# Five small changes of order and grain in a one-core hybrid mixer kernel: Inverse's stores and conversions, the scan's first level, the value rows' load, the opening

## The chip, the cores and the metric

The kernel runs on one core of a Trainium2 chip. The core has a tensor engine (PE) for matmuls and four others: the vector engine (DVE), the scalar engine (ACT), GpSimd (POOL) and the sync engine (SP). Each engine works through its own queue of instructions in the order in which they were written at build time, and waits on semaphores for what other engines deliver. SP, ACT and POOL also issue DMA transfers between the chip's memory (HBM) and the core's own memory; an issued transfer runs by itself on 16 DMA engines that all queues share, but the issuing instruction holds its engine's queue until it is accepted. The metric is the device time of one execution in microseconds (us); lower is better.

## The reference, cut to what matters

One layer over 128 context tokens and 2048 sample tokens of width 1024. The input projection feeds three branches: A, a bidirectional gated delta rule in chunks; B, a spatial-gating MLP; C, a Fourier mixing. Each is gated by a SiLU path, projected, merged with sigmoid gates and projected out.

```python
shift, scale, gate = ada_mod(c, w_ada, b_ada)
xn = rmsnorm(h, ln_g) * (1.0 + scale) + shift
proj = xn @ w_in                       # q k v, beta, decays, z_a, u_b, v_b, z_b, x_c, z_c, gates
# branch A, per chunk and head, both directions:
m = eye + beta * (k @ k.T) * dec_strict
sol = triangular_solve(m, rhs, lower=True, unit_diagonal=True)
s, o = lax.scan(step, s0, ...)         # state passed from chunk to chunk
o_a = rmsnorm(o, o_norm_g) * silu(z_a)
# branch B:
o_b = (u * (w_s @ rmsnorm(v, g_norm) + b_s)) * silu(z_b)
# branch C:
o_c = fft(x_c).real * silu(z_c)
merged = sum(sigmoid(gates_n) * (o_n @ w_branch_n))
y = rmsnorm(h + gate * (merged @ w_out), final_g)
```

## The kernel before, in words

Matmuls in full precision are made of three half-precision ones (high by high, low by high, high by low), so that a weight is split into `whi` and `wlo` and the activations into `xh` and `xl`. All of these go through one helper (`mm`, L239). Tokens are tiled as four tiles of 512 columns and one of 128 (`TBS`).

The work comes in stages: an opening (0 to 42 us), in which the adaLN maps are loaded and summed up; the z_a gate and the normalised activations (to 150 us); the q/k/v projection and the decays (to about 430 us); the spatial gating's v (to about 550 us); U and Z_B, whose product with v makes branch B (to 765 us); the Fourier branch (765 to 1050 us); the merges (to 2010 us); and the output projection. Branch A's work is laid in between these as a background generator, `delta()`. A pacer advances it by one step for each so many microseconds of dense work (`pace.tick`), and a list scheduler that simulates the engines then sets the order on each engine. A matmul of the background therefore stands at a fixed place in PE's queue; if its input is late, all dense work behind it waits. `tc.issue_after(x)` tells the scheduler not to place what follows ahead of the instruction x; on the instruction's own engine this is a matter of order alone.

Branch A goes in five groups of chunks (the context chunk, then four of four). For each chunk `prep` computes products and decays and leaves "late" steps: `late` writes an earlier step's result to HBM from ACT's queue, one step behind. For each group `base_inverse` (called Inverse here) inverts the 32-column base blocks of the triangular matrices, by 31 steps of two DVE operations over `E` (L1094, L1095). It then splits `E`, once straight and once transposed, into high and low halves in `XB`: the high part by ACT (L1100), the low part by DVE (L1101), 128 x 1024 each. The results go to HBM as `ei`, one store per direction: 64 partitions by 32 rows of 256 bytes. For groups 0 to 3 the stores are put in the list `extra`, and the next late step issues all that the list holds, on ACT's queue (L984); what remains at the end goes to SP's (L1407). For the last group SP issues them at once (L1109).

The scan loads `ei` and other results (SP, L1150 to L1156) into `ES`, `N` and others, has POOL copy parts of them (`T`, L1167), and runs the first level of the solve on PE as eight products `ES,N`.

In the gating stage, DVE multiplies each tile of U into a row `vrow` of branch B's values (L1529), POOL multiplies with the gate (`sg`, made by ACT at L1430 and DVE at L1432), and the next row of values is loaded one group ahead. In the Fourier stage `us`, `yT`, `X`, `Y` and `xc` are the transforms' intermediate tiles on ACT, DVE and POOL.

In the opening the order on DVE, ACT and PE is kept as written. `column_sums(b, g)` is one DVE operation over 1024 columns of an adaLN tile that has landed (`ab`), `block_pair` a product of it on PE, `row_copy` ACT's copy of this (`adr`), `turn_rows` PE's transposition of the copy, and `bound(i)` a few small DVE operations that bound the shift (0) or scale (1). `step0` and `step1` advance the first weights' splitting (`zhi`, `zlo`, `wsc`). The end of the opening is `bs` on DVE, then the scale matmul, then the first normalised tile.

Of the kernel before, what the change touches and what calls it, by code (L numbers as in the profile page):

```python
# [14 lines left out]
AF = mybir.ActivationFunctionType  # L15
ALU = mybir.AluOpType
# [19 lines left out]
FS = 4096.0  # L36
VS = 2048.0
ADA_D = (6, 7, 12, 13, 14, 15)
TBS = [(0, 512), (512, 512), (1024, 512), (1536, 512), (2048, 128)]
# [149 lines left out]
def hybrid_flow_kernel(ctx: ExitStack, tc: tile.TileContext, x_prompt, x_sample, state_delta, c, c_ctx, w_ada,  # L189
# [3 lines left out]
    G, SY = nc.gpsimd, nc.sync  # L193
    V, A, PE = [_InTurn(tc, e_) for e_ in (nc.vector, nc.scalar, nc.tensor)]
# [40 lines left out]
    mhalf = sb(cp, [P, 1], "mhalf")  # L235
    G.memset(mhalf, -0.5)

    def mm(out, l, r, start=True, stop=True):
        PE.matmul(out, l, r, start=start, stop=stop)  # L239

    def mm3(out, l, r, start=True, stop=True):

# [275 lines left out]
    def column_sums(b, g):  # L518
        V.scalar_tensor_tensor(spare(1), arrived[b], 1.0, rowc[g], ALU.mult, ALU.mult, accum_out=ada[:, b, g:g + 1])

    def block_pair(b):
        ps = bank(ps_d, [2, 256])
        for k in range(KT):
            mm(ps, scT[:, k, :], arrived[b + k // 4][:, k % 4 * 256:(k % 4 + 1) * 256], k == 0, k == KT - 1)
        return ps

    def turn_rows(b, adr):
        for k in range(2):
            PE.transpose(pa[:, b + k, :], adr[:, k * P:(k + 1) * P], ident[:2, :2])

    def row_copy(ps):
        adr = sb(p0p, [2, 256], "adr", bufs=1)
        A.copy(adr, ps)
        return adr
# [29 lines left out]
    p_ = block_pair(0)  # L564
# [3 lines left out]
    adr = row_copy(p_)  # L568
# [6 lines left out]
    p_ = block_pair(2)  # L575
# [5 lines left out]
    adr = row_copy(p_)  # L581
# [14 lines left out]
    step0()  # L596
    fetch_blocks(8, 9)
    turn_rows(4, adr)
    step0()
    step1()  # L600
    column_sums(13, 1)
    step1()
    step0()
    fetch_blocks(14, 10, 15, 11)
    p_ = block_pair(8)
    step1()
    step1()
    adr = row_copy(p_)
    turn_rows(8, adr)
    bound(0)  # L610
    column_sums(14, 0)
    column_sums(14, 1)
    p_ = block_pair(10)
    column_sums(15, 0)
    column_sums(15, 1)
    adr = row_copy(p_)
    turn_x0(4)
# [355 lines left out]
    def late(pairs=(), made=None):  # L973


        while owed and (made is None or len(owed) > 1):
            with tc.issue_after((made or owed[-1][1]).ins):
                for dst, src in owed.pop(0)[0]:
                    A.dma_start(dst, src)
        if made is not None:  # L980
            owed.append((list(pairs), made))
            with tc.issue_after(made.ins):
                while extra:
                    A.dma_start(*extra.pop(0))  # L984

    extra = []
# [86 lines left out]
    def base_inverse(g):  # L1073
        nt = len(GROUPS[g])
        nb = 16 * nt
        XB = sb(dq, [P, 2048], "XB")
        X, tmp = XB[:, 0:1024], XB[:, 1024:2048]
        E = sb(dq, [P, 1024], "E")
        if nt < 4:
            V.memset(X, 0.0)  # L1080
            V.memset(tmp, 0.0)
        b3 = lambda t_: t_.rearrange("p (j i) -> p j i", j=32)
        for d in range(2):
            SY.dma_start((X if d == 0 else tmp)[64 * d:64 * d + nb, :], ndD[g][d].rearrange("t h (b j) i -> (t h b) (j i)", b=4))
        for _ in range(8):
            yield 0
        V.tensor_copy(b3(X[64:P, :]), tmp[64:P, :].rearrange("p (i j) -> p j i", j=32))
        G.memset(E, 0.0)
        G.memset(E[:, 0:1024:33], 1.0)
        X3, E3 = b3(X), b3(E)  # L1090
        for k in range(31, 0, -1):
            n_ = 32 - k
            t3 = tmp[:, 0:k * n_].rearrange("p (j i) -> p j i", j=k)
            V.tensor_tensor(t3, X3[:, 0:k, k:k + 1].to_broadcast([P, k, n_]), E3[:, k:k + 1, k:32].to_broadcast([P, k, n_]), ALU.mult)  # L1094
            V.tensor_tensor(E3[:, 0:k, k:32], E3[:, 0:k, k:32], t3, ALU.subtract)  # L1095
            if k % 2 == 0:
                yield 1
        both = XB.bitcast(F16).rearrange("p (j l w c) -> p j l w c", j=32, l=2, w=2)
        for w, src in ((0, E3), (1, E.rearrange("p (i j) -> p j i", j=32))):
            A.activation(both[:, :, 0, w, :], src, AF.Copy, scale=FS)  # L1100
            V.scalar_tensor_tensor(both[:, :, 1, w, :], src, FS, both[:, :, 0, w, :], ALU.mult, ALU.subtract)  # L1101
            yield 1
        out = [(eD[g][d].rearrange("j t (y x) -> (t y) j x", x=128),
                both[64 * d:64 * d + nb].rearrange("p j l w c -> p j (l w c)")) for d in range(2)]
        if g < 4:
            extra.extend(out)
        for o_ in out:
            if g == 4:
                SY.dma_start(*o_)  # L1109
            yield 1  # L1110

    odd, wide, q_st, q_hi = [1], [], [], []

# [122 lines left out]
    def scan():  # L1236
# [20 lines left out]
        for _ in range(14):  # L1257
            yield 1
        for i in range(3):
            next(lev)  # L1260
            if i == 1:
                nlev = level(*order[1][::2])
                R2 = next(nlev)
            for _ in range(3):
                yield 1
# [248 lines left out]
    vst = ExitStack()  # L1514
    vp = pool(vst, "vp", 2)
    vnext = sb(vp, [P, NTOK], "vrow")
    SY.dma_start(vnext, vsD[0])
    for g in range(4):
        uw, zw = getw(2, 2)
        vrow = vnext  # L1520
# [366 lines left out]
```

## Time and profile before

| | |
|---|---|
| three runs, us | 2190.08, 2191.36, 2196.57; median 2191.36 |
| the profiled execution | 2189.06 us, of which the profile's span is 2186.8 |
| PE busy | 2108.4 us (96% of the span) |
| DVE, ACT, POOL busy | 1314.1, 1037.0, 704.8 us |
| mean granted clock of PE | 0.99 |
| DMA | 371.89 MB, mean 170 GB/s |

How to read it: times are those of one profiled execution, counted from the span's start. In a row of the timeline the first number is the start, the second the duration, then the engine, the line, the operation with output and inputs, and in brackets how long the engine sat idle ahead of it and who released it. "<-issue" means that the engine waited for nothing that the profile shows; ACTq and SPq are the queues' DMA issues, with the time that the issue took. Several like instructions in a row are one row ("x12"). A line such as L239 can be a helper's, so the tiles' names tell what is meant.

### The profile page before, as it was taken

To read this page: it belongs to the slowest core of one execution; us is meant where nothing else is said; L and a number is where in the kernel's file an instruction comes from. 1 tells how busy PE (TensorE), PEld (TensorE's weight loads), DVE (VectorE), ACT (ScalarE), POOL (GpSimd) and SP (SyncE) were. 2 spreads that over 40 slices of the span, in tenths; PEclk is the share of its full clock that TensorE was granted. 3 is DMA by queue.
4 is the path that set the end of the run, shared out by engine and by line. 5 is a ranking of instruction groups with operands and counts; after the bars stand their busy time and mean duration, and the time that the engine had idled before them with its cause. 6 is when DMAs were issued, how large, how long until landed. Compare 5 with 4: busy or idle time off the path is not lost. (4 is left out here: it accounts for less than half of the span.)

```text
span 2186.8 us, 42541 instructions
## 1 busy us (share of the span) xinstructions
PE 2108.4 (96%) x16249; PEld 1208.5 (55%) x16249; DVE 1314.1 (60%) x3039; ACT 1037.0 (47%) x2378; POOL 704.8 (32%) x869
## 2 busy tenths in 40 slices
PE   7999999999889999899899999899999999999998
PEld 4455444456445677777555555555655444444444
DVE  6656854389779697366665556765564544233454
ACT  5554744476555664445544445655553422223332
POOL 0321332233333432442322223355443222122543
PEclk9999999999999999999999999999999999999999
DMA  8625732277776743434655546766665533433542
GB/s 341 222 76 187 261 112 88 84 228 220 239 225 212 218 153 101 121 123 137 214 163 168 165 156 190 235 200 217 199 199 157 164 125 115 134 101 119 177 149 106
DMA packets 228011, 371.89 MB, mean 170 GB/s; under 512 B 38728, under 2 KB 125152, under 8 KB 225376
## 3 DMA queue, kind: packets, MB, share of 16 engines
q1 hardware_dynamic: 175424, 274.20, 39.9%
q0 software_dynamic: 12688, 51.27, 6.5%
q10 hardware_dynamic: 39696, 43.72, 6.0%
q8 instruction: 127, 2.08, 0.4%
q14 instruction: 76, 0.62, 0.1%
HBM read 241.48 MB, written 127.62 MB: 169 GB/s over the span
## 5 line engine op out<-in xcount | busy, mean ns | idle before, releaser
L239 PE MATMUL b<-xh,whi 128*128 128x512 f16 (+1 forms) x1920 | 650.9, 348 | 8.7 <-DVE sg L1432 6.0
L239 PE MATMUL b<-xl,whi 128*128 128x512 f16 (+1 forms) x1920 | 651.6, 348 | 0.0
L239 PE MATMUL b<-xh,wlo 128*128 128x512 f16 (+1 forms) x1920 | 650.7, 348 | 0.0
L239 PEld LDWEIGHTS <-whi 128*128 128x128 f16 x3904 | 356.3, 98 | 335.7 <-issue 16.6
L239 PEld LDWEIGHTS <-wlo 128*128 128x128 f16 x1952 | 191.3, 98 | 177.1 <-issue 2.8
L239 PE MATMUL b<-big,bhi 128*128 128x512 f16 (+1 forms) x960 | 250.7, 347 | 4.5 <-ACT big L1664 3.1
L1704 POOL TENSOR_TENSOR mrow<-mrow,sg 128x512 f32<-128x512 f32 (+1 forms) x80 | 94.6, 1183 | 281.5 <-DVE sg L1703 172.9
L239 PE MATMUL b<-big,blo 128*128 128x512 f16 (+1 forms) x480 | 162.9, 347 | 0.2 <-DVE blo L310 0.2
L1694 ACT ACTIVATE sg<-b,winv 128x512 f32<-128x512 f32 (+1 forms) x120 | 74.2, 618 | 132.8 <-PE b L239 132.3
L239 PEld LDWEIGHTS <-xh 128*128 128x128 f16 x1496 | 118.3, 99 | 28.9 <-issue 1.8
L239 PEld LDWEIGHTS <-bhi 128*128 128x128 f16 x960 | 86.4, 98 | 80.9 <-issue 4.2
L1703 DVE SCALAR_TENSOR_TENSOR sg<-b,binv,sg 128x512 f32<-128x512 f32 (+1 forms) x80 | 53.4, 667 | 128.5 <-PE b L239 120.3
L934 POOL TENSOR_TENSOR cy<-cy,raw 128x545 f32<-128x545 f32 (+1 forms) x48 | 65.3, 1387 | 183.8 <-ACT raw L933 183.8
L1167 POOL COPY T<-ES 32x256 f16<-32x256 f16 x68 | 28.1, 414 | 206.6 <-DMA ES<-ei 175.9
L239 PE MATMUL b<-wlo,xh 128*128 128x128 f16 x544 | 94.6, 221 | 0.0
L239 PE MATMUL b<-whi,xh 128*128 128x128 f16 x544 | 94.6, 221 | 0.0
L239 PE MATMUL b<-whi,xl 128*128 128x128 f16 x544 | 94.5, 221 | 0.0
L253 DVE CAST wscb<-wss 128x1 bf16<-128x1 f32 x89 | 13.6, 153 | 133.7 <-ACT wlo L297 55.4
L239 PE MATMUL b<-wohi,mh 128*128 128x512 f16 (+2 forms) x248 | 91.9, 372 | 0.0
L239 PE MATMUL b<-wolo,mh 128*128 128x512 f16 (+2 forms) x248 | 91.9, 372 | 0.0
L239 PE MATMUL b<-wohi,ml 128*128 128x512 f16 (+2 forms) x248 | 91.7, 372 | 0.0
L310 DVE SCALAR_TENSOR_TENSOR wlo<-wst,wsc,whi 128x1024 f16<-128x1024 f32 x52 | 70.6, 1360 | 32.7 <-ACT whi L309 32.6
(481 smaller groups left out, 4245.8 us busy)
## 6 DMA issues: line engine op xcount, KB each, us to landing
wst<-in_w_blk_dram SPq DMA_DIRECT2D x58, 512.0 KB, 6.1
qkv<-cy POOLq DMA_DIRECT2D x12, 1089.0 KB, 5.3
st<-br SPq DMA_DIRECT2D x48, 256.0 KB, 3.6
mrow<-mrg SPq DMA_DIRECT2D x18, 512.0 KB, 3.8
mrow<-mrg SPq DMA_DIRECT2D x16, 576.0 KB, 3.9
mrg<-mrow POOLq DMA_DIRECT2D x16, 576.0 KB, 3.8
dc<-dec SPq DMA_DIRECT2D x17, 512.0 KB, 4.7
kq<-qkv SPq DMA_DIRECT2D x34, 256.0 KB, 4.2
```

Of the source, the lines that this page charges most:

```text
L239: PE.matmul(out, l, r, start=start, stop=stop)
L253: V.tensor_copy(sb16, ss)
L310: w.low = V.scalar_tensor_tensor(w.lo, st, s, w.hi, ALU.mult, ALU.subtract)
L934: G.tensor_tensor(y[:, c0:c1], y[:, c0:c1], raw[:, 1 + c0:1 + c1], ALU.mult)
L1167: G.tensor_copy(T16[rows(a0, b), :, :, b], ES[0:32, :, 2 * a0 + b, :, wT])
L1694: A.activation(sg, ps, AF.Sigmoid, scale=gw.inv)
L1703: V.scalar_tensor_tensor(sg, ps, binv[:, 1:2], sg, ALU.mult, ALU.mult)
L1704: G.tensor_tensor(mr, mr, sg, ALU.add)
```

## The change

Five parts. **Opening**: the column sums (13, 1) and (14, 0) and the second advance of the weights' steps are written at other places, and `bound(0)` is written near the end. **Conversions**: each of Inverse's four conversions is made in two halves of 16 of the 32 rows, both kinds for the first half, then both for the second, so that there are four pieces on ACT and four on DVE per group. **Stores**: each store is made in two halves likewise. A late step issues at most one from the list, not all of it; the last group's go out as soon as a half is ready, one direction on SP's queue and the other on ACT's. **Scan**: the first three steps of the first level may not be placed ahead of the newest matmul written so far. **Value rows**: the first load of a row comes tile by tile, in five transfers.

```diff
-        PE.matmul(out, l, r, start=start, stop=stop)
+        newest[0] = PE.matmul(out, l, r, start=start, stop=stop)
...
     turn_rows(4, adr)
+    column_sums(13, 1)
     step0()
     step1()
-    column_sums(13, 1)
-    step1()
-    step0()
     fetch_blocks(14, 10, 15, 11)
     p_ = block_pair(8)
     step1()
+    step0()
+    column_sums(14, 0)
+    adr = row_copy(p_)
     step1()
-    adr = row_copy(p_)
     turn_rows(8, adr)
-    bound(0)
-    column_sums(14, 0)
     column_sums(14, 1)
     p_ = block_pair(10)
+    step1()
     column_sums(15, 0)
+    bound(0)
     column_sums(15, 1)
...
-                while extra:
+                if extra:
                     A.dma_start(*extra.pop(0))
...
-        for w, src in ((0, E3), (1, E.rearrange("p (i j) -> p j i", j=32))):
-            A.activation(both[:, :, 0, w, :], src, AF.Copy, scale=FS)
-            V.scalar_tensor_tensor(both[:, :, 1, w, :], src, FS, both[:, :, 0, w, :], ALU.mult, ALU.subtract)
-            yield 1
-        out = [(eD[g][d].rearrange("j t (y x) -> (t y) j x", x=128),
-                both[64 * d:64 * d + nb].rearrange("p j l w c -> p j (l w c)")) for d in range(2)]
-        if g < 4:
-            extra.extend(out)
-        for o_ in out:
-            if g == 4:
-                SY.dma_start(*o_)
-            yield 1
+        for j0 in (0, 16):
+            js = slice(j0, j0 + 16)
+            for w, src in ((0, E3), (1, E.rearrange("p (i j) -> p j i", j=32))):
+                A.activation(both[:, js, 0, w, :], src[:, js], AF.Copy, scale=FS)
+                V.scalar_tensor_tensor(both[:, js, 1, w, :], src[:, js], FS, both[:, js, 0, w, :], ALU.mult, ALU.subtract)
+                yield 1
+            out = [(eD[g][d][js].rearrange("j t (y x) -> (t y) j x", x=128),
+                    both[64 * d:64 * d + nb, js].rearrange("p j l w c -> p j (l w c)")) for d in range(2)]
+            if g < 4:
+                extra.extend(out)
+            else:
+                SY.dma_start(*out[0])
+                A.dma_start(*out[1])
...
         for i in range(3):
-            next(lev)
+            with tc.issue_after(newest[0].ins):
+                next(lev)
...
-    SY.dma_start(vnext, vsD[0])
+    for t0, tn in TBS:
+        SY.dma_start(vnext[:, t0:t0 + tn], vsD[0][:, t0:t0 + tn])
```

The lines behind the change move by two to five (L1430 becomes L1434, L1101 becomes L1105).

The first place is ACT's queue in the second group's late steps, where the trace of before has the stores at 637 to 648 us. `ei` are Inverse's stores, `n`, `qk` and `kT` the late steps' own, `sg` is a gate of the dense work. Before:

```order
L1063 ACTIVATE n_864_6753<-n_863_6751 128x512
L984 DMA ei_3926<-XB_5743 64x32x128
L979 DMA n_7_3836<-n_857_6689 128x1024
L984 DMA ei_3926<-XB_5743 64x32x128
L1063 ACTIVATE n_870_6795<-n_869_6793 128x512
L979 DMA n_7_3853<-n_859_6704 128x1024
L979 DMA qk_7_3870<-n_864_6753 128x1024
L1430 ACTIVATE sg_6784<-b_6759,winv_5724 128x512
```

And after, at the same place:

```order
L1065 ACTIVATE n_864_6765<-n_863_6763 128x512
L986 DMA ei_3926<-XB_5751 64x16x128
L981 DMA n_7_3836<-n_857_6699 128x1024
L986 DMA ei_3926<-XB_5751 64x16x128
L1065 ACTIVATE n_870_6808<-n_869_6806 128x512
L981 DMA n_7_3853<-n_859_6714 128x1024
L986 DMA ei_3926<-XB_5751 64x16x128
L1434 ACTIVATE sg_6797<-b_6772,winv_5732 128x512
L981 DMA qk_7_3870<-n_864_6765 128x1024
```

Three halves now stand ahead of `sg` where two wholes stood, and one `qk` store has gone behind it; the fourth half follows the last `qk` store, twelve rows further on.

The second place is DVE's queue at the end of the last Inverse, at 873 to 881 us in the trace of before. `yT` are operations of the Fourier stage. Before:

```order
L1094 TENSOR_TENSOR XB_9660<-XB_9660,E_9661 128x31
L1095 TENSOR_TENSOR E_9661<-E_9661,XB_9660 128x31
L1547 TENSOR_SCALAR X_1091_8275<-b_10217,X_1091_8275 128x4x63
L1602 TENSOR_SCALAR X_1091_8275<-X_1091_8275 128x4x63 x2
L1101 TENSOR_SCALAR XB_9660<-E_9661,XB_9660 128x32x32 x2
L1616 TENSOR_TENSOR yT_9544<-b_10238,us_10263 128x7x32
L1617 TENSOR_TENSOR yT_9544<-b_10238,us_10263 128x7x32
L1432 TENSOR_SCALAR sg_10300<-b_10275,zs_9546,sg_10300 128x512
```

And after:

```order
L1096 TENSOR_TENSOR XB_9688<-XB_9688,E_9689 128x31
L1097 TENSOR_TENSOR E_9689<-E_9689,XB_9688 128x31
L1621 TENSOR_TENSOR yT_9569<-b_10266,us_10291 128x7x32
L1622 TENSOR_TENSOR yT_9569<-b_10266,us_10291 128x7x32
L1105 TENSOR_SCALAR XB_9688<-E_9689,XB_9688 128x16x32 x4
L1436 TENSOR_SCALAR sg_10328<-b_10303,zs_9571,sg_10328 128x512
```

The conversions are four pieces instead of two, and `yT` stands ahead of them; `sg` stays behind them.

The third place is PE's queue at the scan's start, 893 to 910 us in the trace of before. Before:

```order
L239 MATMUL b_10536<-xl_94,whi_8874 128x128
L239 LDWEIGHTS wlo_8875
L239 MATMUL b_10536<-xh_93,wlo_8875 128x128
L239 LDWEIGHTS N_1274_10475
L239 MATMUL b_10749<-ES_10477,N_1274_10475 128x32
L239 LDWEIGHTS xh_93
L239 MATMUL b_10572<-whi_9648,xh_93 128x128
```

And after, from 336 rows further on (168 weight loads and 168 matmuls):

```order
L241 MATMUL b_10710<-wlo_9674,xh_93 128x128
L241 LDWEIGHTS xl_94
L241 MATMUL b_10710<-whi_9673,xl_94 128x128
L241 LDWEIGHTS N_1274_10509
L241 MATMUL b_10783<-ES_10511,N_1274_10509 128x32
```

The first of the eight products `ES,N` stood ahead of 168 matmuls of dense work, and the other seven behind them; now all eight stand behind.

More of the change, by code (lines that the diff above doesn't have):

```diff
@@ L236, in hybrid_flow_kernel @@
     G.memset(mhalf, -0.5)
+    newest = [None]
     def mm(out, l, r, start=True, stop=True):
-        PE.matmul(out, l, r, start=start, stop=stop)
+        newest[0] = PE.matmul(out, l, r, start=start, stop=stop)
     def mm3(out, l, r, start=True, stop=True):
```

## The prediction

> **What bounds the kernel now.** I read the busy times first, then the tensor engine's (PE's) waits by stage, then the order of work around each wait. The page's row of busy times says that PE is the bound; the rest of the span, 2186.8 less 2108.4, is 78.4 us in which it is idle.
>
> ```profile
> PE 2108.4 (96%) x16249; PEld 1208.5 (55%) x16249; DVE 1314.1 (60%) x3039; ACT 1037.0 (47%) x2378; POOL 704.8 (32%) x869
> ```
>
> The change leaves PE's matmuls as they are, so it can act only on those 78 us (or add to them). The view of PE's waits, here from 575 to 935 us (rows: total, times, longest), names what it waits for; most of these rows belong to places that the change touches. The two rows after "..." are the same view from 545 to 575 us.
>
> ```profile
> PE b L239 <- DVE sg L1432: 8.6, 3, 5.5
> PE b L239 <- POOL T L1167: 5.0, 1, 5.0
> PE b L239 <- ACT yT L1637: 2.8, 2, 1.9
> PE b L1030 <- DVE tok L1014: 1.8, 1, 1.8
> PE b L239 <- DVE X L1602: 1.2, 1, 1.2
> PE b L1030 <- DVE ss L1004: 0.9, 1, 0.9
> PE b L239 <- POOL X L1601: 0.6, 1, 0.6
> ...
> PE b L239 <- DVE vrow L1529: 2.4, 1, 2.4
> PE b L239 <- DVE T L1032: 1.1, 1, 1.1
> ```
>
> **The change part by part.** Gains are in us of PE's idle time; each has a value and, in brackets, its ends.
>
> Opening order. DVE's column sums (xl<-ab) take 1.2 us each, and four of them run one after the other up to 39.1 us, after which PE's scale matmul still waits for bs:
>
> ```profile
> 27.25 0.16 DVE L182 TENSOR_SCALAR wsc<-b 128x1 int32<-128x1 int32 x1 [2.02 <-PE b L182]
> 32.47 1.28 DVE L182 SCALAR_TENSOR_TENSOR zlo<-wst,wsc,zhi 128x1024 f16<-128x1024 f32 x1 [1.15 <-ACT zhi L182]
> 37.84 1.22 DVE L182 SCALAR_TENSOR_TENSOR xl<-ab,rowc 128x1024 f16<-128x1024 f32 x1
> 40.02 0.16 PE L182 MATMUL b<-bs,ones 128*128 128x1 bf16 x1 [1.20 <-DVE bs L182]
> ```
>
> Two of the four move ahead, into the holes of 2.02 and 1.15 us; the tail is shorter by 2 x 1.22 = 2.4 us, and the three small operations of the first bound move into it (about 0.16 each by the 27.25 row, so 0.5). That leaves 2.0 (0, if the two tiles have not landed by then, to 2.4).
>
> Value rows by tile. The first load of 1088 KB is issued at 551.89; DVE, then idle 5.50 us, gets it at 558.10, and the next two operations on it are followed by two conversions of Inverse, behind which T (L1032) stands:
>
> ```profile
> 551.89 0.33 SPq L1517 DMA_DIRECT2D vrow<-vs  x1
> 558.10 1.41 DVE L1529 SCALAR_TENSOR_TENSOR vrow<-b,winv,vrow 128x512 f32<-128x512 f32 x2 [5.50 <-DMA vrow<-vs]
> 559.42 3.73 DVE L1101 SCALAR_TENSOR_TENSOR XB<-E,XB 128x1024 f16<-128x1024 f32 x2
> st<-br SPq DMA_DIRECT2D x48, 256.0 KB, 3.6
> ```
>
> A piece of 256 KB, the size of the st<-br loads (3.6 us), lands near 555.5, 2.6 us earlier. That covers the whole 2.4; the 1.1 behind T remains in part, since the conversions still stand ahead of T and now begin 2.6 us earlier. Together 2.0 of 3.5 (0 to 3.5): I stay under the sum because the second operation now waits for a second piece. SP issues four rows more, 4 x 0.33 = 1.3 us; the second group's rows, queued behind them, are read only after the first group's five gates, and those cover it.
>
> Stores in halves. At 637 us two stores of 512 KB of Inverse's result (ei, L984), in rows of 256 B, go out on ACT's queue among the late steps' own stores (L979). The issue of a store stands until the queue has room, and what stands behind it on ACT waits:
>
> ```profile
> 637.71 0.67 ACTq L984 DMA_DIRECT2D ei<-XB  x1
> 640.15 1.71 ACTq L984 DMA_DIRECT2D ei<-XB  x1
> 641.98 5.44 ACTq L979 DMA_DIRECT2D n<-n  x1
> 648.23 0.69 ACT L1430 ACTIVATE sg<-b,winv 128x512 f32<-128x512 f32 x1 [5.64 <-issue]
> 649.75 0.59 PE L239 MATMUL b<-xh,whi 128*128 128x512 f16 x1 [5.49 <-DVE sg L1432]
> 638.00:644.00 6.00, 6.00 (x70) 4.84 (x69) 3.25 (x5) 2.48 (x5) 0.76 (x1) 1.00 0.83 123
> ```
>
> So a gate (sg) that was ready waited 5.64 us behind an issue, and PE 5.49. After the change three halves stand ahead of sg and the fourth behind it, after the last qk. The window's last column gives 123 GB/s while the stores ran, hence 256 KB/123 = 2.1 us a half. Three halves from 637.71 are through by 644.1, against 646.3 for four; and an issue is let go before its data is through, so sg should start at 643 to 644 instead of 648.2. PE wants its result at 649.75 - 5.49 = 644.26, DVE's step between; I take 4.7 (0, if the third half stands as long as the store at 641.98, to 5.5).
> At 736 us the same happens in the next group:
>
> ```profile
> 736.38 4.62 ACTq L984 DMA_DIRECT2D ei<-XB  x2
> 741.18 3.17 ACTq L979 DMA_DIRECT2D n<-n  x1
> DMA to landing us min/median/max: 2.4/3.5/4.9
> ```
>
> Here PE pays only the 1.8 of tok, which ACT's delay hands on through DVE: 1.5 (0 to 1.8). In the third group (823 us) PE does not wait; two halves now go to SP's queue after prep's end, ahead of the load that feeds the last Inverse. Taken at nothing, as the conversions of that Inverse come only at 874; if it is late all the way, 2 x 2.1, which the new waits below take in. A rule speaks against halves: the Trainium skill, "DMA: Bandwidth & Descriptors", section Bandwidth, advises at least 1 MiB a transfer, since each carries a fixed part. By the formula of that page's anatomy section (2.0 us and bytes over 436 GB/s, fitted on the other kind of queue) a half is an estimated 2.6 us, three are 7.8, and this term would be 3.3 for 4.7, the sum 1.4 smaller. The trace has 3.5 us as the median landing of a whole (the page's estimate 3.2), so the page is close there; for a half no row exists.
>
> Conversions in four pieces. DVE's and ACT's conversions of Inverse's result, ten of 1024 columns each, become twenty of 512:
>
> ```profile
> L1101 DVE SCALAR_TENSOR_TENSOR XB<-E,XB x10: 1225/1906/1949, 559.4 to 876.8; 128x1024 f16<-128x1024 f32 x10
> 811.72 2.93 ACT L1100 ACTIVATE XB<-E 128x1024 f16<-128x1024 f32 x2
> 814.67 1.91 DVE L1101 SCALAR_TENSOR_TENSOR XB<-E,XB 128x1024 f16<-128x1024 f32 x1 [0.64 <-ACT XB L1100]
> 815.13 0.83 PE L239 MATMUL b<-cf,Y 128*128 128x128 f16 x12 [1.87 <-ACT yT L1637]
> 818.26 0.39 PE L239 MATMUL b<-cf,X 128*128 128x128 f16 x2 [1.18 <-DVE X L1602]
> 876.81 1.92 DVE L1101 SCALAR_TENSOR_TENSOR XB<-E,XB 128x1024 f16<-128x1024 f32 x1 [0.66 <-ACT XB L1100]
> 881.79 0.37 ACT L1612 COPY us<-b 128x256 f32<-128x256 f32 x1
> 881.16 0.29 PE L239 MATMUL b<-cf,X 128*128 128x128 f16 x2 [2.64 <-DVE sg L1432]
> 882.39 1.44 PE L239 MATMUL b<-cf,Y 128*128 128x128 f16 x12 [0.94 <-ACT yT L1637]
> ```
>
> At 811 to 818 ACT's yT stood behind 2.93 us of conversions and DVE's X behind 1.91; PE lost 0.93 + 1.87 + 0.62 + 1.18 = 4.6 (ss, yT, POOL's X, DVE's X). In the new order us, yT, X and T come before the conversions on ACT, and yT, X and T before them on DVE: 3.2 (0 to 4.6), since ss doesn't move and the last X still follows. At 876 to 882 PE lost 2.64 + 0.94 = 3.6. There yT comes ahead of the four pieces, but sg stays behind them, and a wait is added: ACT's queue issues two halves itself, the second only when DVE's fourth piece is done; sg stands between the two, X, us and the yT that PE waits for behind both. DVE's conversions end now at 876.81 + 1.92 = 878.7; if the four pieces end there too, that yT comes after four operations of ACT of about 0.4 (the us row), near 880.4 and not 882.4; PE's sg comes earlier than that. Less 0.5 for a fourth piece that ends later, 1.5 (-1, if ACT waits long for it, to 3.6). Pieces of 512 columns should take the 0.70 of a vrow operation (1.41/2), so 2.8 a group against 2 x 1.225: 0.35 more, 0.7 in the two groups where PE waits; in the others DVE's idle time hides it.
>
> Scan's first level. Its first matmul stands ahead of 168 dense ones that don't need it, and waits for the loads of the scan, POOL's copy last:
>
> ```profile
> 897.96 0.84 POOL L1167 COPY T<-ES 32x256 f16<-32x256 f16 x2 [3.48 <-DMA ES<-ei]
> 898.81 0.18 PE L239 MATMUL b<-ES,N 128*128 128x32 f16 x1 [4.96 <-POOL T L1167]
> 910.05 0.33 PE L239 MATMUL b<-ES,N 128*128 128x32 f16 x7
> ```
>
> Put behind those 168 (898.81 to 910.05, 11.2 us), it is reached at 898.81 - 4.96 + 11.2 = 905.1, 6.3 us after the copies end at 898.8. The wait goes: 5.0 (0 to 5.0). PE's arrival may move ahead of the loads by all that the 811 to 882 stretch gains, 4.7, before it is late again.
>
> New waits. The order of ACT, DVE and SP shifts by some places from 550 to 880 us. Nothing in the trace shows what then comes last; between no wait and three of the size of tok's 1.8 I take one, 1.8.
>
> Sum: 2.0 + 2.0 + 4.7 + 1.5 + 3.2 + 1.5 + 5.0 = 19.9, less 0.7 and 1.8: 17.4. The profiled execution took 2189.06 us (2.3 outside its span) and would come to 2171.7; it lies 2.3 under the median of the three runs, 2191.36, from which I count: 2174.0.
>
> **The rivals.**
> The halves stand as long as wholes: three at the 3.5 us of a whole end at 637.71 + 10.5 = 648.2, where sg starts now, and both store terms (6.2) are gone: 2180.2. For it speaks that the bytes and their 256 B rows stay the same, against it the 123 GB/s.
> The conversions' waits come back under other names, the 4.7 of 811 to 882 gone: 2178.7. For it: sg still stands behind four pieces; against it: yT and X don't. With the first rival together: 2184.9.
> The first level doesn't move or waits again: 2179.0. For it would speak loads later by over 6.3 us; SP's half-stores of group 3 come ahead of them, at 2.1 each too little.
> Slower: every half on ACT's queue is paid by PE in full. There are twelve large ones (4, 4, 2, 2); at 2.1 each 25.6 us instead of the 5.5 + 1.8 paid now, +18.3, against 11.2 from the other terms (after the 2.5 of costs): 2198.5. It decides from (7.3 + 11.2)/12 = 1.5 us paid per half. The 5.64 row speaks for it; against it, that the 640.15 issue took 1.71 with PE still covered, and that work of ACT's own now lies between the halves.
>
> **How the numbers follow.** Forecast 0.55; stores 0.14, conversions 0.12, both 0.06, first level 0.06, slower 0.07. Best ends together give 26.4, 2165.0; the range goes to 2164 and up past both rivals to 2188, which leaves out the slower case. No change that can be told is 0.3%, 6.6 us: both rivals together fall on that line, and with a tail of the others it gets 0.08; slower 0.07, faster 0.85.
>
> **What would show it.** PE's wait for sg near 650 under 1 us; ACT's gap before sg without an issue of 5 us; PE's row for ES,N without a wait for POOL; vrow's wait under 3 us on DVE; bs on DVE 2 us earlier; less than 2 us of waits for yT and X before each of the last two Inverse ends. Wrong would be an n or ei issue over 3 us on ACT with sg behind it, a wait of PE above 2 us with a new releaser between 550 and 890, or ES copies that end after PE's 168 matmuls.

## The result, and the profile after

Twenty runs of each kernel: 2190.03 us before (2184.19 to 2196.57) and 2180.49 us after (2174.15 to 2186.51), medians. The ratio is 0.9954, with a 95% interval of 0.9944 to 0.9964, so the change saves 10 us (8 to 12), where 17.4 were forecast. The profiled execution of the changed kernel took 2174.15 us, the fastest of its twenty; its trace, with a span of 2172.3 us, lies 14.5 us under that of before, and some 5 us of this are that execution's luck.

Where the 14.5 us come from is seen in the view of busy times by stretch. After the stretch and its length stands PE's busy time; the last three columns are the granted clock, the DMA share and GB/s. First the kernel before, then the changed one:

```profile
0.00:45.00 45.00, 33.02 (x171) 18.65 (x172) 24.08 (x59) 22.21 (x40) 2.59 (x10) 0.97 0.94 361
45.00:545.00 500.00, 494.00 (x3118) 256.77 (x3117) 331.41 (x610) 274.93 (x524) 139.39 (x165) 0.99 0.49 165
545.00:935.00 390.00, 360.93 (x3407) 245.65 (x3406) 293.93 (x733) 207.03 (x583) 137.65 (x181) 0.97 0.59 180
935.00:1680.00 745.00, 720.37 (x6915) 448.72 (x6914) 450.35 (x1163) 383.20 (x999) 270.75 (x375) 1.00 0.58 181
```
```profile
0.00:45.00 45.00, 36.27 (x181) 20.26 (x182) 26.67 (x63) 24.97 (x44) 2.54 (x10) 0.96 0.97 387
45.00:545.00 500.00, 495.17 (x3135) 257.98 (x3134) 333.55 (x626) 275.85 (x538) 140.96 (x168) 1.00 0.49 166
545.00:935.00 390.00, 368.21 (x3569) 250.00 (x3568) 299.13 (x749) 212.41 (x595) 141.51 (x191) 0.99 0.59 182
935.00:1680.00 745.00, 718.77 (x6803) 444.66 (x6801) 446.42 (x1150) 379.21 (x985) 269.01 (x367) 1.00 0.59 181
```

PE's idle time is the length less the busy time. It falls from 18.0 to 13.6 us up to 545 us, from 29.1 to 21.8 from 545 to 935, and rises from 31.3 to 34.1 after that (the rest of the span included): 78.4 before, 69.4 after, 9.0 less. The other 5.5 us are busy time, 2108.4 before and 2102.9 after for the same 16249 matmuls. That is the clock, and it was no term of the prediction, which let the change act on the 78 us of idle time only: the third row's granted clock is 0.97 before and 0.99 after. It isn't this pair alone: the mean granted clock is 0.994 over the twenty runs of the changed kernel, and 0.990 over those of the kernel before that ran beside the later experiments. The kernel before in steps of two us behind its stall at 650 shows how:

```profile
648.00:650.00 2.00, 0.25 (x1) 0.10 (x1) 0.77 (x2) 1.77 (x10) 0.22 (x1) 0.50 1.20 329
650.00:652.00 2.00, 2.00 (x6) 0.76 (x5) 1.49 (x3) 2.00 (x10) 1.90 (x2) 0.50 0.81 297
652.00:654.00 2.00, 2.00 (x8) 0.67 (x6) 1.11 (x3) 2.00 (x6) 1.97 (x4) 0.61 0.77 184
654.00:656.00 2.00, 2.00 (x11) 0.94 (x10) 0.16 (x1) 0.90 (x4) 1.69 (x4) 1.00 0.96 313
```

After this wait PE's clock is granted at half, and stays low for some 4 us after work has come back: 6 matmuls in two us, then 8, then 11. Busy time times the clock that was missing, 2.00 x 0.50 + 2.00 x 0.39 and so on, gives 1.9 us for this stall on top of its 5.5. Added up over the span this is 15.9 us before, in eight places, and 8.0 after, in five; from 545 to 935 us it is 8.4 and 3.3. This working takes all busy time as slowed by the clock, which is an estimate; its 7.9 less is somewhat more than the 5.5 by which the busy time fell.

What PE waits for from 545 (in this view 575) to 935 us after the change:

```profile
PE b L241 <- DVE sg L1436: 3.3, 4, 1.6
PE b L999 <- issue: 3.2, 1, 3.2
PE b L241 <- ACT yT L1642: 2.8, 1, 2.8
PE b L241 <- DVE T L1034: 2.0, 3, 1.1
PE b L999 <- DVE n L1047: 1.7, 1, 1.7
PE b L241 <- DVE X L1607: 1.1, 2, 0.6
PE b L241 <- DVE yT L1622: 1.0, 1, 1.0
```

The 5.5 us for sg (now 0.47 there) and the 5.0 for POOL's T are gone. A wait of 3.2 has come, and 2.8 for yT stand where 2.6 for sg stood. The stores themselves do what was forecast, at 633 to 639 us:

```profile
633.01 0.67 ACTq L986 DMA_DIRECT2D ei<-XB  x1
634.42 1.22 ACTq L986 DMA_DIRECT2D ei<-XB  x1
636.99 1.63 ACTq L986 DMA_DIRECT2D ei<-XB  x1
638.66 0.69 ACT L1434 ACTIVATE sg<-b,winv 128x512 f32<-128x512 f32 x1 [2.29 <-PE b L241]
638.69 2.49 ACTq L981 DMA_DIRECT2D qk<-n  x1
```

ACT's gate sg no longer waits for an issue but for PE's own matmuls; PE then waits 0.47 us for it, not 5.49. The store that stands longest, qk with 2.49, has sg in front of it.

### The profile page after: what moved, and what is told of

It is laid out like the page before. It is cut to its first block, busy times and chain, and to the rows that moved or that the text cites. A ratio compares the mean times of both kernels' runs of the same rounds, so it can differ in the third digit from the quotient of the medians.

```text
span 2172.3 us, 42588 instructions
## 1 busy us (share of the span) xinstructions
PE 2102.9 (97%) x16249; PEld 1204.3 (55%) x16249; DVE 1314.2 (60%) x3049; ACT 1037.8 (48%) x2388; POOL 704.2 (32%) x869
```

## The experiments

All ratios are to runs of the kernel before on the same chip, with 95% intervals. The table gives, beside the median of each kernel's runs, the time of its one profiled execution and two readings of that execution from 545 to 935 us: PE's idle time, and the time lost to the half clock, worked out as above (where the windows start moves this by up to 0.4). Where the profiled execution lies far from the median, the two readings are those of an uncommonly fast or slow one.

| kernel | median, us | ratio | profiled, us | idle | lost to the clock |
|---|---|---|---|---|---|
| before | 2190.0 | | 2189.1 | 29.1 | 8.4 |
| opening alone | 2188.4 | 0.9997 (0.9985 to 1.0008) | 2183.1 | 29.3 | 6.9 |
| value rows alone | 2191.0 | 1.0001 (0.9990 to 1.0011) | 2190.8 | 27.1 | 9.1 |
| scan's first level alone | 2190.0 | 1.0004 (0.9993 to 1.0014) | 2191.2 | 28.9 | 8.1 |
| conversions alone | 2196.5 | 1.0029 (1.0017 to 1.0041) | 2190.4 | 31.4 | 7.1 |
| stores alone | 2180.8 | 0.9960 (0.9948 to 0.9971) | 2180.8 | 20.4 | 1.7 |
| the whole change | 2180.5 | 0.9954 (0.9944 to 0.9964) | 2174.2 | 21.8 | 3.3 |
| the whole change again | 2177.4 | 0.9945 (0.9925 to 0.9965) | 2170.9 | 20.9 | 1.5 |
| stores and conversions | 2181.2 | 0.9959 (0.9944 to 0.9973) | 2188.9 | 25.7 | 4.6 |
| whole, without the conversions | 2186.4 | 0.9979 (0.9966 to 0.9991) | 2184.9 | 23.5 | 8.5 |
| whole, halves on two queues | 2178.5 | 0.9953 (0.9938 to 0.9967) | 2178.2 | 22.2 | 2.9 |
| whole, last stores whole | 2176.4 | 0.9944 (0.9926 to 0.9961) | 2175.3 | 21.6 | 1.6 |
| whole, last halves on SP | 2186.0 | 0.9974 (0.9958 to 0.9990) | 2186.6 | 27.4 | 5.1 |
| whole, two queues and last whole | 2180.2 | 0.9953 (0.9938 to 0.9969) | 2183.9 | 23.2 | 4.0 |

The parts don't add: only the stores, made alone, save time that can be told, and they save nearly all of it; the conversions, made alone, cost 6 us (4 to 9).

**The opening alone.**

```diff
     turn_rows(4, adr)
+    column_sums(13, 1)
...
-    bound(0)
-    column_sums(14, 0)
...
     column_sums(15, 0)
+    bound(0)
```

> Only the opening's order is changed. First theory (the tail of column sums is shorter by two, and all behind it moves up): the first normalised matmul starts 2.0 us earlier than before (42.6 to about 40.6), and the time is 2 us less. Rival (the z_a stage behind it is paced by transfers, so the gain is given back): the same 2.0 us at 42 us, but PE's waits for DMA or DVE between 45 and 150 us grow by as much, and the time is the same.

Measured: the first normalised matmul starts at 40.1 us, not 42.6, 0.5 of it because the first transfers landed earlier; in the changed kernel it is 39.9. The rival's z_a stage doesn't take it back: PE's idle time up to 545 us is 15.1 us here and 18.0 before, and has a mean of 15.1 (13.5 to 16.3) in the eight profiles with the new order and 17.0 (15.1 to 18.8) in the six without. Later in this kernel's trace the waits for yT grew (4.4 us at 831, 2.8 at 896). The time doesn't tell 2.0 us from none. What follows: the opening's 2 us are there at 42 us and, in the mean, still at 545; whether they last to the end is not settled.

**The value rows alone.**

```diff
-    SY.dma_start(vnext, vsD[0])
+    for t0, tn in TBS:
+        SY.dma_start(vnext[:, t0:t0 + tn], vsD[0][:, t0:t0 + tn])
```

> Only the first row of values is loaded tile by tile. First theory (after the changed kernel's trace): vrow's wait of 2.4 us goes, but T, behind Inverse's conversions, becomes the wait: 0 to 1 us less. Rival (the prediction's): both together fall from 3.5 to 1.5 us: 2 us less.

Measured: vrow's wait is gone, T's waits are 0.93 and 0.64; the two together fall from 3.5 to 1.6. The time is the same; 1.9 us is below what its interval can tell. In the changed kernel it is 2.0 that remain, again T's:

```profile
556.21 0.23 PE L241 MATMUL b<-T 128*128 128x128 f16 x1 [1.59 <-ACT T L1033]
557.43 0.77 PE L241 MATMUL b<-T 128*128 128x128 f16 x11 [0.45 <-DVE T L1034]
```

A new wait of 1.06 us at 574, for tok behind an operation of Inverse on DVE, comes with the conversions and not with this part: it stands in all eight profiles with conversions in pieces and in none of the six without. What follows: the wait moved to T, as the prediction said of a part of it; 1.5 to 1.9 of the 3.5 us are saved on the spot, and the time can't show whether they last.

**The scan's first level alone.**

```diff
-            next(lev)
+            with tc.issue_after(newest[0].ins):
+                next(lev)
```

> Only the scan's first level is kept behind the newest matmul. First theory: the wait of 5.0 us for POOL's copy goes, and with it the slow clock after it (168 matmuls took 11.2 us behind the wait, 9.4 at the full rate): 5 to 7 us less. Rival (the scan starts later and pays it back in its own chain): the waits for ACT's S and R between 900 and 1700 us grow by 3 us or more, and the time is 0 to 3 us less.

Measured: neither. The wait for POOL's T is gone, and 5.1 us for yT stand in its place, at the same moment:

```profile
888.76 0.34 SPq L1251 DMA_DIRECT2D skn<-kv  x1
896.25 0.49 DVE L1330 TENSOR_SCALAR S<-S,usc 128x512 f32<-128x512 f32 x1 [2.33 <-DMA S<-in_state_delta_dram]
899.14 0.29 PE L241 MATMUL b<-whi,xh 128*128 128x128 f16 x1 [5.12 <-DVE yT L1620]
```

The first operations of the scan on ACT and DVE (v, then S) wait for the scan's loads, which SP issues from 888.8 on, and in their queues the Fourier stage's us and yT stand behind them. PE was moved past one thing that waits for these loads, and met the next. Moreover, with the other four parts in place, the order of every engine is the same with this edit and without it: the dense work then stands ahead of the first level anyhow. So this part does nothing in the whole change: the two built programs are the same. The later waits that the rival expected can't be told either: PE's idle time from 935 to 1680 is 26.6 us here and 24.6 before, and lies between 23.6 and 27.8 in all profiles.

**The conversions alone.**

```diff
+        for j0 in (0, 16):
+            js = slice(j0, j0 + 16)
...
+                A.activation(both[:, js, 0, w, :], src[:, js], AF.Copy, scale=FS)
```

> Only the conversions are made in four pieces per group; the stores stay whole, on ACT's queue at one late step, and on SP's for the last group. First theory (what PE waits for at 811 to 818 and 876 to 882 goes over to other rows of the same two places, as in the changed kernel's trace, 4.6 to 2.9 and 3.6 to 3.4; the stall at 650 stays): 0 to 2 us less. Rival (the prediction's): 3 to 5 us less, with these two places under 4 us together.

Measured: 6 us slower. The two places fell as the prediction had it (876 to 882: 3.6 to 0.5; 811 to 818: 4.6 to 2.9), together 3.3 us as the rival said, and the scan's start cost far more:

```profile
890.31 0.68 PE L239 MATMUL b<-ES,N 128*128 128x32 f16 x8 [12.00 <-DMA N<-n]
```

All eight products now stand ahead of the dense work (presumably because the scheduler's simulation takes the scan to be ready earlier; no run shows the reason). The loads come when they did, 8.4 us after the last conversion, and PE stands for 12 us. Neither theory had this. But the profiled execution is the fastest of nine, 6 us under their median, with a total of 2.3 us more idle time than before in this stretch: the trace shows the stall, and not where the median's 6 us go.

**The stores alone.**

```diff
-                while extra:
+                if extra:
                     A.dma_start(*extra.pop(0))
...
+        for j0 in (0, 16):
+            js = slice(j0, j0 + 16)
+            out = [(eD[g][d][js].rearrange("j t (y x) -> (t y) j x", x=128),
```

> Only the stores of Inverse's results are halved and spread over the late steps; conversions stay whole, and the last group's stores stay on SP's queue. First theory: PE's wait for sg near 650 us falls from 5.5 to under 1 us, tok's 1.8 near 750 goes, and nothing of like size comes: 5 to 7 us less. Rival (the order that the scheduler makes of it brings new waits, as the 3.2 us near 752 in the changed kernel's trace): the wait for sg goes, but waits of 3 us or more come between 680 and 760, and the time is 2 to 4 us less.

Measured: 0.9960, 8.8 us less. sg's wait near 642 is 1.05; the rival's new wait is there too (3.8 near 755). Yet the saving is above both forecasts (the interval, 6.4 to 11.4, touches the first), since the waits at 811 to 818 fell to 2.7 and the scan's start to 0.8 as the order moved. The scan's loads start as late as before here (8.4 us after the last conversion), but yT stands ahead of the scan's S on DVE. In this stretch 6.7 us of slow clock went too; over the whole span, though, PE's busy time is only 0.7 us less than before (2107.7), as slow clock came in other places, 2.8 us near 948 among them. What follows: this part carries the gain, half of it directly (4.4 of the 5.5 at 650), the rest mainly through the order that comes out of it; the clock's share stays open.

**The whole without the conversions.**

```diff
+        for w, src in ((0, E3), (1, E.rearrange("p (i j) -> p j i", j=32))):
+            A.activation(both[:, :, 0, w, :], src, AF.Copy, scale=FS)
```

> The changed kernel with whole conversions (two per engine and group); stores in halves, opening, value rows as changed. First theory (the gain is the stores' and the opening's; four pieces bring nothing of their own once the order is what it is): within 2.5 us of the changed kernel beside it. Rival (the pieces let yT and X through ahead of the conversions, the prediction's 4.7 us): 3 to 5 us more than the changed kernel.

Measured: 9 us more by the medians than the changed kernel beside it, 7 by the ratios, and 5.9 more than the changed kernel's first twenty runs: at or above what the rival forecast. But its cause is not what shows. At the places named in it nothing got worse by more than 0.6 us: 811 to 818 has 2.9 here as in the changed kernel, and 875 has 3.9 against 3.4. In this order a store, qk, came to stand ahead of sg instead:

```profile
642.08 2.96 ACTq L981 DMA_DIRECT2D qk<-n  x1
645.09 0.69 ACT L1436 ACTIVATE sg<-b,winv 128x512 f32<-128x512 f32 x1 [5.38 <-issue]
646.61 0.38 PE L241 MATMUL b<-xh,whi 128*128 128x512 f16 x1 [3.03 <-DVE sg L1438]
```

and PE waited 4.1 us at 574, where the copy into XB stood on DVE, idle 6.89 us for its load, and 2.5 for yT at 890. What follows: halves alone don't clear ACT's queue; it matters that no long issue stands ahead of what PE waits for, and one place in ACT's order is worth 2 to 2.6 us (3.03 against 0.47 and 1.08 in the two profiles of the changed kernel).

**Stores and conversions, without the other parts**, and **the changed kernel again**.

> Only the stores in halves and the conversions in pieces; opening, value rows as before, no order set for the scan's first level. First theory (the opening brings its 2.0 us also in the whole; the value rows nothing; the place of the first level comes out of the stores and conversions by themselves): the first level stands behind the dense work here too, and the time is 2 us, or with the value rows up to 3, more than the changed kernel's. Rival (what is won in the opening is lost later): the changed kernel's time within 1 us.

> The changed kernel once more, for a second profiled execution and for comparison with the three beside it on one chip. First theory (executions differ in when transfers land, and two waits stand directly behind a load: the one for the copy into XB near 752 and the one for the scan's state and v near 884): these two rows differ between the two profiles by 1 us or more together, all other waits by less than 0.5 each; 2177 to 2183 us. Rival (executions differ by the granted clock alone): the waits are the same within 0.5 us, and PE's busy time differs by 3 us or more.

Measured: 2181.2 (2175.3 to 2188.9) and 2177.4 (2170.9 to 2184.7); the ranges and the intervals of the ratios overlap, so what the opening and the value rows bring in the whole stays open: 3 us by the ratios, anything from a loss of 2 to a gain of 8 if the two intervals are combined. The first level does stand behind the dense work in the smaller kernel. Between the two profiles of the changed kernel the wait near 752 went from 3.2 to 1.6 and yT's near 884 from 1.0 to 0.5; the other waits agree within 0.5 but for a new 1.2 at 668, 0.6 more at 641 and at 675, and 0.7 less at 570. So the waits behind loads do differ between executions. PE's busy time differs by 2.2 us, and over 26 runs time and granted clock go together (correlation -0.60). The two are linked in part: the 3.2 us near 752 were followed by half clock (1.6 us lost), the 1.6 by none. Both theories hold a part, and neither all of its marks.

**Halves on two queues.** The wait near 752 was put down to XB. In the changed kernel the fourth half goes out at 739.8, the next group's load into XB, which must wait for it, at 743.4, and DVE's copy of what was loaded holds up the operations behind it, for one of which PE waits (which one is inferred; PE's row names no releaser):

```profile
739.77 0.60 ACTq L986 DMA_DIRECT2D ei<-XB  x1
743.40 2.43 SPq L1086 DMA_DIRECT2D XB<-nd  x2
749.95 1.05 DVE L1089 COPY XB<-XB 64x1024 f32<-64x1024 f32 x1 [3.86 <-issue]
752.54 0.63 PE L999 MATMUL b<-cst,qr 128*128 128x128 f32 x4 [3.21 <-issue]
```

```diff
                 if extra:
                     A.dma_start(*extra.pop(0))
+                if extra:
+                    SY.dma_start(*extra.pop(0))
```

> The changed kernel, but a late step issues two halves, one on ACT's queue and one on SP's, so that four halves are out after two late steps. First theory (the wait of 3.2 us near 752 comes from XB: the fourth half goes out late, so that the load of the next group into XB starts late, DVE waits for it at the copy L1089, and PE for what stands behind that on DVE): the load of XB is issued 3 us or more earlier against PE's work around it, the wait near 752 falls under 1 us, the one for sg near 640 stays under 1.5 us, and the time is 2 to 4 us under the changed kernel's (ratio to the kernel before near 0.994). Rival (the wait at 752 is the scheduler's order and hangs on nothing in XB): the load comes earlier and the wait stays at 3 us; the time is the changed kernel's within 1.5 us.

Measured:

```profile
731.23 0.60 ACTq L986 DMA_DIRECT2D ei<-XB  x1
736.53 1.13 SPq L1088 DMA_DIRECT2D XB<-nd  x2
741.28 1.05 DVE L1091 COPY XB<-XB 64x1024 f32<-64x1024 f32 x1 [2.12 <-DMA XB<-nd]
752.77 0.66 PE L1001 MATMUL b<-cst,kq 128*128 128x128 f32 x4 [0.57 <-DVE n L1049]
```

The load is 6.9 us earlier, the copy 8.7. The qr matmul, now at 756, doesn't wait; the 0.57 of kq is the largest wait left there, and 0.56 with the same edit in the last kernel below, against 1.6 to 4.6 in the seven other profiles with halved stores: the cause is shown. sg's wait near 643 is 0.30. The time, though, is the changed kernel's: waits of 2.4 and 1.8 us for POOL's X came near 862 and 876, 2.4 for qr at 573 (1.8 and 1.1 in the changed kernel) and 1.0 for T at 747.

**The last group's stores**, in two ways: all four halves on SP, whose edit is shown, or one whole store per direction on SP behind all four pieces.

```diff
-                A.dma_start(*out[1])
+                SY.dma_start(*out[1])
```

> The changed kernel, but all four halves of the last group's stores go out on SP's queue. First theory (ACT's second issue, which waits for DVE's fourth piece, holds up X, us and the yT that PE waits 2.8 us for near 871): that wait falls to 1.5 us or less, the scan's loads start at most 1 us later, and the time is 0 to 1.5 us less than the changed kernel's. Rival (yT waits for sg and X on DVE anyway): the wait stays at 2.5 us or more, and the time is the same or 1 us more.

> The changed kernel, but the last group's stores go out whole, one per direction, both on SP's queue after all four pieces, as in the kernel before. First theory (the 5 us that the scan's start cost came from the loads that wait until the last store has read XB; the place in PE's queue only says which wait shows it): the loads of the scan (skn, sv) are issued 2 us or more later against PE's work, a wait of 2 to 5 us for yT, S or POOL's T comes at the scan's start, and the time is 1.5 to 4 us more than the changed kernel's. Rival (the new place of the first level behind the dense work is what took the wait away): no wait over 1.5 us there, and the changed kernel's time within 1 us.

Measured: with the halves on SP the wait for yT near 876 is 1.23, but X before it costs 1.62, so the place gains only 0.5; and 4.7 us for yT come at the scan's start, and 4.6 near 755 where the changed kernel has 3.2 and 1.6. These are the waits of one execution of a kernel that spreads widely: its runs go from 2175.4 to 2192.5, and five of the twelve lie under 2181. With the stores whole these 4.7 are 0.9, though the loads start later: 8.6 us after the last conversion (870.7 to 879.3), against 7.5 with the halves on SP and 6.3 in the changed kernel. The order of two operations on DVE tells why. Halves on SP:

```profile
889.12 0.49 DVE L1331 TENSOR_SCALAR S<-S,usc 128x512 f32<-128x512 f32 x1 [2.63 <-DMA S<-in_state_delta_dram]
889.52 0.59 DVE L1621 TENSOR_TENSOR yT<-b,us 128x256 f32<-128x256 f32 x1
890.60 0.29 PE L241 MATMUL b<-whi,xh 128*128 128x128 f16 x1 [4.67 <-DVE yT L1622]
```

Stores whole:

```profile
884.15 0.59 DVE L1622 TENSOR_TENSOR yT<-b,us 128x256 f32<-128x256 f32 x1
885.23 0.23 PE L241 MATMUL b<-whi,xh 128*128 128x128 f16 x1 [0.91 <-DVE yT L1623]
885.67 0.48 DVE L1332 TENSOR_SCALAR S<-S,usc 128x512 f32<-128x512 f32 x1 [0.50 <-DMA S<-in_state_delta_dram]
```

yT stands behind S, which waits for a load, in the first, and ahead of it in the second. So the theory that the loads' start alone sets the stall fell: what the order puts behind the loads counts. The changed kernel has the bad order (S, then yT) and early loads, and pays 0.98; that the early loads are what spares it is likely, but no run moves them alone.

**Both edits together.**

> The changed kernel with both edits that did not cost time: two halves per late step, one on ACT's queue and one on SP's, and the last group's stores whole on SP's. First theory (both take away a wait of their own): near 752 under 1.5 us, at the scan's start under 1.5 us, and 2 to 4 us less than the changed kernel beside it. Rival (each is the scheduler's order by chance, and the two don't add): the changed kernel's time within 2 us, with a wait of 2 us or more in a new place between 690 and 900.

Measured: 0.9953; 0.56 near 752 and nothing at the scan's start, but 2.4 and 3.6 us for POOL's X near 862 and 877. The rival held in its waits, and in its time against the changed kernel's first twenty runs (it is 2.8 us above the six beside it): no version tried is told apart from the changed kernel for the better; the one with the last stores whole has the lowest median, within its interval.

## Why the prediction came out as it did

The direction and the range held, and the size was 10 us where 17.4 stood. In the pair of traces, from 545 to 935 us, PE's idle time can be booked step by step; the first row, the opening, lies before this stretch.

| step | forecast | in the pair of traces |
|---|---|---|
| opening | 2.0 | 2.3 (42.58 to 39.91, less 0.4 of earlier transfers) |
| stores at 650 | 4.7 | 5.0 (5.49 to 0.47) |
| stores at 750 (tok) | 1.5 | 1.8 (gone) |
| conversions, 811 to 818 | 3.2 | 1.7 (4.60 to 2.94) |
| conversions, 876 to 882 | 1.5 | 0.2 (3.58 to 3.35) |
| value rows | 2.0 | 1.5 (3.50 to 2.04) |
| scan's start | 5.0 | 4.0 (4.96 to 0.98) |
| T at 703, not named | 0 | 0.7 |
| new waits and longer pieces | -2.5 | -7.4 (3.2, 1.6, 1.1 and smaller) |

- **The opening's step was right at its place.** The first normalised matmul came earlier by what was forecast, and the means up to 545 us (15.1 and 17.0) bear it out.
- **The stores' step was right**, in size and mechanism, at 650 us: the third half's issue ended 5.6 us after the first began (633.01 to 638.62), where 5.3 to 6.3 were forecast, and sg then waited for PE and not for ACT's queue. Its rival, halves that stand as long as wholes, needed 10.5 us and fell. Its 3.5 us was misread, besides: this is the median landing of the scan's loads `ES<-ei`, and the profile of before has no landing for the stores, so that the formula is close to a whole's landing isn't shown either. The formula of the Trainium skill, "DMA: Bandwidth & Descriptors", section Anatomy of one DMA, gives an estimated 2.6 us for a half and 7.8 for three, by which sg would still be late. Here sg was not late, though the one half on ACT's queue whose landing the profile shows took 3.5 us, more than that estimate: an issue ended before its data was through (1.63 us was the longest of the three), so the issues and not the landings set when sg could start.
- **"New waits" was the term that failed**, 1.8 for what was 7.4. (The table's -2.5 has the longer pieces too; DVE's conversions take 16.8 us in all where they took 16.3.) Its bound, three waits of the size of tok's, came from waits that existed; the change made a longer one. The 3.2 near 752 and the 1.6 near 694 come with the stores (3.8 and 2.0 in stores alone), the 1.1 near 574 with the conversions. The prediction asked what stands behind the fourth half on ACT; it did not ask who waits for the fourth half to have read XB. Spreading the stores over late steps sends the last one later, and the next group's load into the same tile with it.
- **The scan's step was near in its sum and wrong in its mechanism.** The edit alone moved the wait to yT, and in the whole it changes no order at all. The 4.0 came out of the order that the stores bring (0.8 is left in stores alone, with yT ahead of S); in the changed kernel S stands ahead of yT, and the loads start 2.2 us earlier after the last conversion (8.4 to 6.3).
- **The conversions' step failed in its mechanism at both places.** At 811 to 818 yT and X did get ahead, and T took over with 1.07. But the same is gained without pieces: 2.7 us are left in stores alone and 2.9 in the whole without the conversions, as here. So this gain belongs to the order that the stores bring. Near 871 next to nothing was gained, and not for the wait that was feared, ACT's second half ahead of X:

```profile
869.03 0.74 DVE L1436 SCALAR_TENSOR_TENSOR sg<-b,zs,sg 128x512 f32<-128x512 f32 x1
869.14 0.59 ACTq L1113 DMA_DIRECT2D ei<-XB  x1
869.83 0.39 ACT L1551 ACTIVATE X<-b 128x260 f16<-128x260 f32 x1 [0.93 <-DVE sg L1436]
870.71 0.83 PE L241 MATMUL b<-cf,Y 128*128 128x128 f16 x12 [2.83 <-ACT yT L1642]
```

The issue is over at 869.73, and X waits until 869.77 for DVE's sg, which stands behind the four pieces; with the halves on SP's queue the place gained only 0.5. The rival "the waits come back under other names" held for this place, by the reason that the prediction gave it: sg still stands behind four pieces. Made alone, this part was a loss, which the prediction had not thought of.
- **The clock had no term.** That the change could act on the idle time only was wrong. With the waits at 650, 816, 882 and 897 went 8.3 us of half-rate work, and the waits at 752 and 871 brought 3.2 back. This partly made up for the new waits: without it the saving would have fallen further short of 17.4, so some of the forecast's nearness is luck.
- **The slower rival** fell: no half on ACT's queue was paid by PE in full.
- After 935 us the scan's and merges' waits gave back 2.8 us in this pair; over all profiles PE's idle time from 935 to 1680 lies between 23.6 and 27.8 us without relation to the change, so this is no effect that can be told.

## What to carry to other kernels

When a wait is taken away, look in each queue for the next thing behind the same late transfer, and price the reuse of the tile: a store that is spread out frees its buffer later, and the load into it moves too. Where a scheduler sets the order, parts of a change don't add, and one place in a queue can be worth 2 to 7 us of a stall (3.03 against 0.47, 4.67 against 0.91, 12.00 against 4.96); test the parts alone and taken out, and don't credit a part with a gain that stays when the part is taken out. A stall of the bound engine of 2 us or more mostly cost its length here and 1.3 to 3 us more at the half clock.

## What the hardware showed that was not expected

The half clock comes after waits that are not one gap: at 811 to 818 us in the kernel before four waits of 0.6 to 1.9 us, 4.6 together within 7 us, were followed by 6 us at half clock (0.50 from 818 to 824), 2.9 us lost; in the changed kernel 2.83 and 0.52 near 871 were enough, while 2.4 us of waiting for POOL's X near 862 brought it as well in the kernel with halves on two queues. The length of a wait alone doesn't decide it: a wait of 3.78 us that ended at 755.5 in stores alone was followed by a clock of 1.00, one of 2.07 that ended at 844 in the kernel with the scan's edit alone by 0.50 (1.7 us lost). The Trainium skill, "TensorE: Matmul & The Clock Gate", Why this matters for your kernels, tells authors to allow no idle gap over about 3 us; the trace agrees on the halving, and shows it after shorter waits too, single ones and ones that lie close together.
